# A second buffer for the blocks of RWKV's inverses, and the modulation's weights in pieces of 512 columns

## The chip, the cores and the metric

The kernel runs on one core of one Trainium2 chip. The metric is the device time of one execution in microseconds (us); the numbers given are medians over runs. A core has a matrix engine (PE), three engines for elementwise work (DVE, ACT, POOL), and a queue on SP that issues most of the transfers (DMA) between DRAM and the on-chip memory. Each engine, and SP too, takes its instructions in a fixed order: an instruction that waits holds back all that stand behind it on its engine.

## The reference, cut to what matters

A network of two layers over 1280 tokens (256 of context, 1024 of latents) of width 1024. For each layer:

```python
mod = silu(cond) @ ada_w[i] + ada_b[i]             # shifts, scales and gates: "the modulation"
h = rmsnorm(x, norm1_g) * (1 + sc1) + sh1
z = h @ w_in[i]                                    # split into four groups
mix = concat(s5(z0), rwkv7(z1), retention(z2), gla(z3)) @ w_out[i]
x = x + g1 * mix
x = x + g2 * (relu(rmsnorm(x, norm2_g) * (1 + sc2) + sh2) @ mlp_w1) ** 2 @ mlp_w2
```

`rwkv7` is a recurrence over tokens, forward and backward, in four heads of 64. Its step is `s = s * w + (s @ a) b^T + v k^T`, `y = s @ r`. In the first layer the modulation of the second layer's first part is computed as well.

## The kernel before, in words

A layer runs in stages: norm 1; the input projection (beside the parameters of S5 and its scans); **the mixers' stage**; output projection, norm 2 and MLP. In the trace the mixers' stage lies at about 462 to 1050 us (first layer) and 2498 to 3055 us (second layer). The rest is mostly dense matrix work.

In the mixers' stage three generators are interleaved by `merge`, each at a share of the matrix engine's estimated time: the modulation (`ada`), RWKV (`rw.run()`), and retention followed by the gated linear attention (`ret_run`, `gla_run`).

RWKV works in chunks of 128 tokens. A "pair" is one chunk forward and one backward; there are ten pairs in a layer. A pair enters `unit1` every six rounds (elementwise preparation, transposes, scores `TE` and `TO`), then `inv` is emitted for the pair, and twelve rounds after `unit1` comes `unit2`, so that `unit2` of one pair and `unit1` of the pair two places later are emitted side by side. `inv` solves 32 triangular blocks of 32x32. Its steps, with their lines:

- L514: four stores of blocks of `TE` and `TO` to a DRAM tile `S` (two buffers);
- L518: one load of `S`, four copies side by side, into the tile `B` (512 KB, **one buffer**);
- L523: a constant into `Yv` (two buffers);
- L527, L528: 31 steps of two small POOL instructions each, `rw_tmp <- rw_Yv, rw_B` and `rw_Yv <- rw_Yv, rw_tmp`;
- L531: four stores of `Yv` to a DRAM tile `S2`; L534: four loads of `S2` into `DT`, the inverse's blocks, which the first matmul of `unit2` (`psu <- rw_R, rw_DT`) multiplies by.

All these transfers stand in SP's queue, together with the loads of RWKV, retention, the gated linear attention and the modulation's weights.

`ada(i, q, pool, bufs)` makes 16 column tiles of the modulation: 8 rows of tiles by 4 column groups of 512. Each of its 16 steps (two for a row) loads one 128x1024 tile of `ada_w` (512 KB; L1517) into one of two buffers and runs two matmuls of 512 columns on it. In the mixers' stage `ada` is run three times in the first layer (48 steps) and twice in the second (32 steps). Its sums stay in the one PSUM bank of the kind `fi` until its last step.

The order on each engine is not that of the program's text: the program is built with `schedule_with_timeline_sim=True`, which lays out each engine's instructions by a simulated timeline. In the trace, instructions of `inv` on POOL alternate with those of the other generators.

Of the kernel before, what the change touches and what calls it, by code (L numbers as in the profile page):

```python
# [16 lines left out]
SEQ = 1024  # L17
# [9 lines left out]
def _consts():  # L27
# [44 lines left out]
    dt = (i[None, :] - i[:, None]).astype(f)            # t - s  # L72
# [9 lines left out]
    ang = np.stack([(tt // 64).astype(f)[:, None] * inv, (tt % 64).astype(f)[:, None] * inv], 1)   # [SEQ, 2, 16]  # L82
# [14 lines left out]
# per-layer small parameters, one column block each (layout only)  # L97
# [3 lines left out]
def _cols(a):  # L101
    """[n*128] -> [128, n]"""
    a = np.asarray(a)
    return np.ascontiguousarray(a.reshape(-1, 128).T)
# [19 lines left out]
def lay_s5(inp, i):  # L124
    """[128, 4*512+64]: B (re; im), B (im; re), C (re; im), C (im; re) by state, and d on the diagonal of its group"""
    g = lambda n: np.asarray(inp[n][i])
    br, bi = (g(n).transpose(2, 0, 1, 3).reshape(64, 512) for n in ("s5_b_re", "s5_b_im"))
    cr, ci = (g(n).transpose(3, 0, 1, 2).reshape(64, 512) for n in ("s5_c_re", "s5_c_im"))
    d = g("s5_d").reshape(4, 4, 16)
    dl = np.zeros((4, 32, 4, 16), np.float32)  # L130
    for p in range(16):
        dl[:, p, :, p] = d[:, :, p].T
    return np.concatenate([np.concatenate([a, b], 0) for a, b in ((br, bi), (bi, br), (cr, ci), (ci, cr))]
                          + [dl.reshape(128, 64)], 1)
# [13 lines left out]
class Pe:  # L148
    """the tensor engine, with an estimate of the time of what it was given (ns)"""
# [18 lines left out]
class K:  # L168
# [29 lines left out]
    def psum(self, **rings):  # L198
        """the banks of PSUM, shared out among kinds of users; b: the others"""
# [16 lines left out]
# ---------------------------------------------------------------- RWKV-7  # L216
def rw_mix(k, j, z, zm, mu, omu):
    """zm = z + mu*(shifted - z) for the 128 columns of tile j; z, zm [128, T]"""
# [42 lines left out]
RW_ROWS = 13            # rows of the spilled columns: v chunks swapped 2, kk 2, r 2, k 2, lo 1, v 2, v reversed by chunk 2  # L261


def rw_store(k, st, sm, omu, zrw, j, zt):
    """token shift of the 128 columns of tile j (zt [128, T]) and what the scans take from them, to DRAM;
    a generator: the parts that need the tensor engine come after the first step"""
# [45 lines left out]
class Rwkv:  # L312
    """zrw: DRAM [128, RW_ROWS, T] as rw_store leaves it; out(p, ps) takes the transposed output of 128 tokens"""

    R, LAT, NP = 6, 12, 3         # rounds between pairs, to their second part, pairs at a time
# [8 lines left out]
    def setup(self):  # L324
# [12 lines left out]
        # states and buffers with fixed zeros  # L337
# [15 lines left out]
        # by chunk: the first direction's output; what the normalized output is multiplied by, and what is added then  # L353
# [7 lines left out]
    def unit1(self, p, d, pr):  # L361
        """elementwise preparation, transposes, scores of 128 tokens in one direction"""
# [17 lines left out]
        def rev(ap):        # [.., 128] reversed in time for the backward direction  # L380
            return ap[..., ::-1] if d else ap

        def v4(ap):         # [128, 2, 128] -> [128, 2, c, 64]
# [11 lines left out]
        # V (scan order, chunks swapped), token-major, into its place beside the chunk updates  # L395
# [11 lines left out]
        ec = self.ec[u["n"] % 2]        # decay from a chunk's start to before and, one column later, after a token  # L407
# [3 lines left out]
        # ar: (r~ 0 | a~ 0 | a~ 1 | r~ 1); a~ in scan order, r~ in natural order within its chunk  # L411
# [6 lines left out]
        # bk: (b_ 0 | k_ 0 | k_ 1 | b_ 1); b = 2*kk*a (its factor -1/2 comes with the masks), k_d  # L418
# [7 lines left out]
        # r~ by keys, and the chunks' decays  # L426
# [13 lines left out]
        u["R"] = R = t("R", [128, 4, 2, 64], 5)      # (v | k) columns  # L440
        A.copy(R[:, :, 1, :], pv[:, 0:256].rearrange("p (h x) -> p h x", h=4))
        # scores: chunk 0 rows (b|k), columns (r~|a~); chunk 1 rows (k|b), columns (a~|r~)
        # TE: (end-of-chunk keys | r~ | a~), TO: (a~ | r~ | end-of-chunk keys)
# [5 lines left out]
        ps2 = [k.ps("u1"), k.ps("u1")]      # the halves of the array's rows work side by side  # L449
# [21 lines left out]
        # Aak V  # L471
# [9 lines left out]
    def gate(self, p, zin):  # L481
        """factor and addend of the normalized output, token-major: ln_g * g and (ln_b + bonus) * g"""
# [23 lines left out]
    def inv(self, pr):  # L506
        """(I - B)^-1 for strictly upper triangular 32x32 blocks: block (unit, head, block) on 4 partitions,
        rows i = 4 i' + j on the j-th"""
        k, nc, w = self.k, self.k.nc, self.w
        S = k.dram.tile([8, 4, 32, 32], F32, name="rw_S", bufs=2)      # (unit, head), block  # L510
# [5 lines left out]
        B = w.tile([128, 32, 32], F32, name="rw_B", bufs=1)  # L516
# [12 lines left out]
        S2 = k.dram.tile([8, 4, 8, 4, 32], F32, name="rw_S2", bufs=2)      # (unit, head), block, i', j, t  # L529
# [52 lines left out]
    def chain(self, u, act):  # L582
        """state pass and outputs of 128 tokens in one direction"""
# [52 lines left out]
    def run(self):  # L636
        """generator over the whole layer: in rounds, a pair of units (one in each direction) enters every R rounds and
        its second part LAT rounds later, when the inverses are there"""
# [27 lines left out]
def rr(gens, width=9):  # L666
    """round robin over generators, at most width at a time, in order; one that yields n sits out n rounds"""
# [17 lines left out]
def pipe(gens, R, width=9):  # L685
    """round robin over generators, of which one more enters every R rounds; one that yields n sits out n rounds"""
# [18 lines left out]
def rsqrt_small(k, y, x):  # L705
    """y = x^(-1/2) for tiles [128, 4], x > 0, without a table"""
# [3 lines left out]
def head_norm_gate(k, w, pre, py, g, lngh, out, p):  # L710
    """RMS norm over each head of py [128 tokens, 256] (PSUM), times ln_g and silu(g); lngh = ln_g/2"""
# [27 lines left out]
# ---------------------------------------------------------------- gated linear attention  # L739
class Gla:  # L740
    """DRAM: q [128 (head, key), T], alo [16, T], vg [T, 512] (v | g), and by chunk kc [128, NCH, 385]: keys times dk^-1/2 (given),
    sums of log decays (times 16; pb, one more column, and bf)"""
# [14 lines left out]
    def update(self, d, n, p, kh, v):  # L757
        """compact state of direction d after its n-th chunk p, from keys kh"""
# [16 lines left out]
    def expand(self, d, sc):  # L775
        """block diagonal over heads"""
# [5 lines left out]
    def chunk(self, p):  # L782
# [11 lines left out]
        if need:  # L794
            g = self.load("g", self.vg[tk, 256:512])
            L = t("L", [128, 14, 128], 2)          # exponents, then factors, of keys and queries by level
# [86 lines left out]
    def run(self):  # L883
# [6 lines left out]
        # log decays (times 16): min(y, 0) - ln(1 + exp(-|y|)), then prefix sums within chunks of 128:  # L890
        # bf inclusive, forward; pb exclusive, backward (one more column: the chunk's sum)
        self.bl, self.dec = t("bl", [128, 2, NCH]), t("dec", [128, 2, NCH])      # the chunks' decays and their exponents
# [33 lines left out]
# ---------------------------------------------------------------- retention  # L926
class Parts:
    """small tiles cut from one [128, n]"""
# [10 lines left out]
def ret_decays(k, w, dl, work):  # L939
    """log(sigmoid(dl)) for a tile [128, n] with equal rows: min(x,0) - 2*atanh(e/(2+e)), e = exp(-|x|)"""  # L940
# [5 lines left out]
    V.tensor_tensor(ax, ax, dl, op=OP.min)                  # -|x|  # L946
# [3 lines left out]
    V.tensor_tensor(u, u, e, op=OP.mult)                    # in [0, 1/3]  # L950
# [11 lines left out]
def exp_acc(k, work, out, x, pre):  # L962
    """exp(x) for small tiles to float32 accuracy, x clamped to [-87, 88]"""
# [19 lines left out]
def rope(k, st, x, p, o):  # L983
    """axial rotation of 128 latents' queries or keys x [128, 256] (4 heads) -> o"""
    V = k.nc.vector
    x = x.rearrange("p (h f a) -> p h f a", h=4, f=4)            # f: (half, x1|x2)
# [11 lines left out]
class Ret:  # L998
    """z: DRAM [T, 1024] (q | k | v | g), q and k rotated; dl [128, 8] decay logits (d, h)"""
# [13 lines left out]
    def update(self, d, n, kk, v):  # L1013
        """state of direction d (block diagonal by pair) before its chunk n+1"""
# [26 lines left out]
    def chunk(self, p):  # L1041
# [22 lines left out]
        AT = t("AT", [128, 2, 2, 128], 2)       # h2, pair  # L1064
# [22 lines left out]
    def run(self):  # L1087
# [12 lines left out]
        # decay within a chunk, both directions, times dk^-1/2: DM[s, h, t]  # L1100
# [9 lines left out]
        # factors of queries GQ[(h2, key), d, pair, t] = g^(t+1 | 128-t), of values GV[s, d, h] = g^(127-s | s)/8;  # L1110
        # gC[d, h] = g^128
# [15 lines left out]
        # states before the n-th chunk of a direction: [(h2, key), pair, (h2, v)], block diagonal in h2  # L1127
# [8 lines left out]
# ---------------------------------------------------------------- S5  # L1136
class S5:
    """u: DRAM [128 (s, p), 16, 160]: row p of each group at token 8c+s"""
# [14 lines left out]
    def params(self):  # L1153
        """state decays, powers, and the three matrices of 8-token steps, kept in DRAM"""
# [21 lines left out]
        V.tensor_scalar(sh, sh, 2.0, None, op0=OP.mult)             # 1 - cos  # L1176
# [5 lines left out]
        V.scalar_tensor_tensor(re, e1, 1.0, th, op0=OP.add, op1=OP.mult)        # expm1  # L1182
# [16 lines left out]
        # powers 0..8  # L1199
# [9 lines left out]
        # with the sign of the half: (-, +) and (+, -) of im; (+, -) of re  # L1209
# [9 lines left out]
        # unit phase of 8 steps, and its decay  # L1219
# [10 lines left out]
        # b_bar (re; im) and (im; re)  # L1230
# [15 lines left out]
        for d0 in range(0, 32, 4):  # L1246
# [26 lines left out]
            # lag matrices, group 4*gq + j at partitions 32j  # L1273
# [738 lines left out]
def merge(k, gens):  # L2012
    run(merged(k, gens))
# [41 lines left out]
```

## Time and profile before

| what | value |
|---|---|
| median of three runs | 3920.55 us (3920.0 to 3921.86) |
| span of the profiled execution, first to last instruction | 3930.7 us (its own time is given by this span alone) |
| PE busy | 3589.8 us (91%) |
| DVE, ACT, POOL busy | 2222.0, 1475.3, 1353.2 us (57%, 38%, 34%) |
| the chain that ended last | PE 64%, POOL 9%, DMA 9%, DVE 8%, ACT 5% |

The chain of waits is followed back from the last instruction: at each step to what released it, or to the instruction before it on its engine. Busy shares are means over stages with different limits; what a change in the mixers' stage is worth is to be read from that stage.

### The profile page before, as it was taken

Reading aid. Unit: us, or ns where it says so; the run is one execution under the profiler, and the core shown is the slowest. Engines: PE = TensorE matmul, PEld = TensorE weight load, DVE = VectorE, ACT = ScalarE, POOL = GpSimd, SP = SyncE. Lnnn points to the kernel's source line nnn. Section 1 sums busy time; section 2 is a strip of 40 time slices with the busy share of each in tenths; the row PEclk is TensorE's granted clock in tenths of the full one; section 3 lists DMA queues with packets and bytes.
Section 4 is the critical chain, followed back from the end, with each engine's and each line's share of the span. In section 5 each row is a group of like instructions: output and inputs, shape, how many; then the busy total and the mean of one; then the engine's idle time right before and its main releaser. Section 6 shows DMA issues by size and latency. Waiting matters only on the chain.

```text
span 3930.7 us, 61448 instructions
## 1 busy us (share of the span) xinstructions
PE 3589.8 (91%) x23136; PEld 2973.0 (76%) x23136; DVE 2222.0 (57%) x4654; ACT 1475.3 (38%) x2980; POOL 1353.2 (34%) x2690
## 2 busy tenths in 40 slices
PE   6999888888799999999998999788888799999997
PEld 2998766577687888888886987667677678888885
DVE  5875456667555444444448875555667464444445
ACT  4266345755433111111214365346655332111222
POOL 1541256567431111111111451266676321111112
PEclk8999988787799999999999999898778899999998
DMA  5434575532521111111103434663423411111111
GB/s 184 149 111 145 163 210 141 168 92 61 163 89 33 33 44 33 43 33 44 33 27 120 146 115 144 180 177 112 111 73 96 141 54 49 49 43 43 49 53 43
DMA packets 369241, 372.84 MB, mean 95 GB/s; under 512 B 97360, under 2 KB 313104, under 8 KB 368688
## 3 DMA queue, kind: packets, MB, share of 16 engines
q1 hardware_dynamic: 333600, 343.08, 28.8%
q10 hardware_dynamic: 35344, 25.83, 2.1%
q8 instruction: 183, 3.00, 0.3%
q14 instruction: 114, 0.93, 0.1%
HBM read 285.18 MB, written 83.63 MB: 94 GB/s over the span
## 4 chain that ended last, share of the span: by engine, by line
PE 64%; POOL 9%; DMA 9%; DVE 8%; ACT 5%; issue 3%; SPq 1%; ACTq 0%; DVEq 0%; POOLq 0%
PE psb L161 56%; PE psu L161 5%; POOL rw_Yv L528 3%; POOL rw_tmp L527 3%; DMA rw_B<-rw_S 2%; DMA rw_S<-rw_Yv 1%; PE pss L161 1%; PE psfi L161 1%; DMA ada_w<-in_ada_w_dram 1%; DVE s_W L1158 1%; PE psch L161 1%; DVE n_h L1579 1%; DMA gl_v<-z_gvg 1%; DVE w_lo L1478 1%; DVE zm L223 1%
## 5 line engine op out<-in xcount | busy, mean ns | idle before, releaser
L161 PE MATMUL psb<-hh,w_hi 128*128 128x512 f32 (+1 forms) x1784 | 664.6, 374 | 12.9 <-ACT hh L1951 4.5
L161 PE MATMUL psb<-hl,w_hi 128*128 128x512 f32 (+1 forms) x1784 | 662.5, 372 | 6.5 <-DVE hl L1581 6.5
L161 PE MATMUL psb<-hh,w_lo 128*128 128x512 f32 (+1 forms) x1784 | 659.5, 371 | 0.0
L161 PE MATMUL psb<-mh,w_hi 128*128 128x512 f32 (+1 forms) x1600 | 601.2, 377 | 20.1 <-ACT w_hi L1475 15.3
L161 PE MATMUL psb<-mh,w_lo 128*128 128x512 f32 (+1 forms) x1600 | 598.3, 375 | 6.6 <-DVE w_lo L1478 6.6
L161 PE MATMUL psb<-ml,w_hi 128*128 128x512 f32 (+1 forms) x1600 | 600.5, 375 | 0.0
L1932 DVE SCALAR_TENSOR_TENSOR x<-psb,mod,x 128x512 f32<-128x512 f32 (+1 forms) x640 | 436.9, 694 | 273.8 <-PE psb L161 273.0
L1478 POOL TENSOR_TENSOR w_lo<-w_raw,w_hi 128x1024 fp32r<-128x1024 f32 x84 | 215.0, 2560 | 765.2 <-ACT w_hi L1475 574.8
L1950 DVE TENSOR_TENSOR hr<-hr 128x512 f32<-128x512 f32 x160 | 150.5, 941 | 513.6 <-ACT hr L1949 513.5
L1949 ACT ACTIVATE hr<-psb 128x512 f32<-128x512 f32 x160 | 88.7, 555 | 862.7 <-PE psb L161 861.8
L161 PEld LDWEIGHTS psb<-hh,w_hi 128*128 128x128 f32 x1784 | 338.6, 190 | 77.7 <-issue 6.0
L161 PEld LDWEIGHTS psb<-hl,w_hi 128*128 128x128 f32 x1784 | 338.0, 190 | 72.7 <-DVE hl L1581 11.0
L161 PEld LDWEIGHTS psb<-hh,w_lo 128*128 128x128 f32 x1784 | 337.5, 189 | 61.2 <-issue 1.4
L1952 POOL TENSOR_TENSOR hl<-hr,hh 128x512 fp32r<-128x512 f32 (+1 forms) x80 | 95.3, 1191 | 795.0 <-ACT hh L1951 502.9
L161 PEld LDWEIGHTS psb<-mh,w_hi 128*128 128x128 f32 x1600 | 303.7, 190 | 81.1 <-ACT w_hi L1475 17.4
L161 PEld LDWEIGHTS psb<-mh,w_lo 128*128 128x128 f32 x1600 | 303.3, 190 | 67.9 <-DVE w_lo L1478 8.2
L161 PEld LDWEIGHTS psb<-ml,w_hi 128*128 128x128 f32 x1600 | 303.4, 190 | 60.3 <-issue 2.9
L1475 ACT CAST w_hi<-w_raw 128x1024 fp32r<-128x1024 f32 (+1 forms) x208 | 212.8, 1042 | 317.8 <-PE psb L161 268.5
L527 POOL TENSOR_TENSOR rw_tmp<-rw_Yv,rw_B 128x60 f32<-128x60 f32 (+24 forms) x620 | 206.1, 332 | 198.6 <-DMA rw_B<-rw_S 100.0
L161 PE MATMUL psb<-w_hi,hh 128*128 128x256 f32 (+1 forms) x928 | 266.0, 290 | 4.8 <-ACT w_hi L1475 4.7
L161 PE MATMUL psb<-w_lo,hh 128*128 128x256 f32 (+1 forms) x928 | 266.9, 288 | 0.6 <-DVE w_lo L1478 0.6
L161 PE MATMUL psb<-w_hi,hl 128*128 128x256 f32 (+1 forms) x928 | 266.2, 288 | 0.0
(469 smaller groups left out, 6710.2 us busy)
## 6 DMA issues: line engine op xcount, KB each, us to landing
w_raw<-in_mlp_w_dram SPq DMA_DIRECT2D x128, 512.0 KB, 3.6
ada_w<-in_ada_w_dram SPq DMA_DIRECT2D x96, 512.0 KB, 4.4
w_raw<-in_w_in_dram SPq DMA_DIRECT2D x40, 512.0 KB, 5.6
w_raw<-in_w_out_dram SPq DMA_DIRECT2D x32, 512.0 KB, 5.2
rw_zin<-z_rw SPq DMA_DIRECT2D x20, 576.0 KB, 5.9
rw_B<-rw_S SPq DMA_DIRECT2D x20, 512.0 KB
z_rw<-zm SPq DMA_DIRECT2D x14, 640.0 KB, 3.1
x<-in_xT_dram SPq DMA_DIRECT2D x4, 2048.0 KB
```

What stands on the lines that cost most here:

```text
L161: return self.t.matmul(out, lhsT, rhs, **kw)
L223: nc.vector.scalar_tensor_tensor(dst[p0:p1], src[p0:p1], mu[p0:p1, j:j + 1], dst[p0:p1], op0=OP.mult, op1=OP.add)
L527: eng.tensor_tensor(o, bc(Yv[:, 0:m, s:s + 1], [128, m, n]), bc(B[:, s:s + 1, s + 1:32], [128, m, n]), op=OP.mult)
L528: eng.tensor_tensor(Yv[:, 0:m, s + 1:32], Yv[:, 0:m, s + 1:32], o, op=OP.add)
L1158: T_ = lambda o, a, b, op: V.tensor_tensor(o, a, b, op=op)
L1475: nc.scalar.copy(hi[:, :n], raw[:, :n])
L1478: e.tensor_tensor(lo[:, :n], raw[:, :n], hi[:, :n].bitcast(F32), op=OP.subtract)
L1579: nc.vector.scalar_tensor_tensor(h, x[:, kt], g[:, kt, cond:cond + 1], r[:, :n], op0=OP.mult, op1=OP.mult)
L1932: V.scalar_tensor_tensor(self.x[b][:, dt_], ps[:, :n], mod[:, 40 + dt_, cnd:cnd + 1], self.x[b][:, dt_], op0=OP.mult, op1=OP.add)
L1949: A.activation(r[:, :n], ps[:, :n], AF.Relu)
L1950: V.tensor_tensor(r[:, :n], r[:, :n], r[:, :n], op=OP.mult)
L1952: (G if j else V).tensor_tensor(hl[:, j, :n], r[:, :n], hh[:, j, :n].bitcast(F32), op=OP.subtract)
```

## The change

`B` gets two buffers. `ada` gets a parameter `wide`, the columns of one loaded tile. At its old default of 1024 it does what it did (the first call, ahead of the layers, keeps it). In the mixers' stage it is called with 512: every matmul has its own tile and its own load of 256 KB, still in two buffers. A step still holds two matmuls, so it now holds two loads and uses both buffers. In on-chip memory `B` takes 4 KB more of each partition, and the `ada_w` tiles 4 KB less. The diff also takes out comments, which is left out here; two lines are added inside `ada`, so that lines behind it stand two further down.

```diff
-        B = w.tile([128, 32, 32], F32, name="rw_B", bufs=1)
+        B = w.tile([128, 32, 32], F32, name="rw_B", bufs=2)
...
-    def ada(self, i, q, pool, bufs=2):
+    def ada(self, i, q, pool, bufs=2, wide=1024):
...
                 if j % 2 == 0:
                     yield
-                    w = pool.tile([128, 1024], F32, name="ada_w", bufs=bufs)
+                if j * 512 % wide == 0:
+                    w = pool.tile([128, wide], F32, name="ada_w", bufs=bufs)
                     c = q * 2048 + j * 512
-                    nc.sync.dma_start(w, self.I["ada_w"][i, kt * 128:kt * 128 + 128, c:c + 1024])
-                k.pe.matmul(ps[32 * j:32 * j + 2, :], self.cs[:, kt], w[:, j % 2 * 512:j % 2 * 512 + 512],
+                    nc.sync.dma_start(w, self.I["ada_w"][i, kt * 128:kt * 128 + 128, c:c + wide])
+                o = j * 512 % wide
+                k.pe.matmul(ps[32 * j:32 * j + 2, :], self.cs[:, kt], w[:, o:o + 512],
                             start=kt == 0, stop=kt == 7)
...
-        merge(k, [(chain([self.ada(a, q, w, 2) for a, q in ad]), ADAW * len(ad)), ...
+        merge(k, [(chain([self.ada(a, q, w, 2, 512) for a, q in ad]), ADAW * len(ad)), ...
```

## Rows read from the trace of the kernel before

**Rows 1.** The page: span; the chain's share by line.

```profile
span 3930.7 us, 61448 instructions
...
PE psb L161 56%; PE psu L161 5%; POOL rw_Yv L528 3%; POOL rw_tmp L527 3%; DMA rw_B<-rw_S 2%; DMA rw_S<-rw_Yv 1%; PE pss L161 1%; PE psfi L161 1%; DMA ada_w<-in_ada_w_dram 1%; DVE s_W L1158 1%; PE psch L161 1%; DVE n_h L1579 1%; DMA gl_v<-z_gvg 1%; DVE w_lo L1478 1%; DVE zm L223 1%
```

**Rows 2.** Busy time by stretch: PE, PEld, DVE, ACT, POOL; clock; DMA share; GB/s.

```profile
462.00:1050.00 588.00, 491.34 (x4978) 392.56 (x4978) 386.03 (x1031) 319.72 (x862) 370.19 (x1002) 0.81 0.49 142
2498.00:3055.00 557.00, 454.92 (x4434) 372.86 (x4434) 357.26 (x939) 294.93 (x798) 345.34 (x950) 0.81 0.45 127
```

**Rows 3.** Waits, both stages: us in total, times, longest.

```profile
POOL rw_tmp L527 <- DMA rw_B<-rw_S: 43.1, 6, 9.0
...
POOL rw_tmp L527 <- DMA rw_B<-rw_S: 56.9, 8, 9.8
```

**Rows 4.** Chain of waits in order of time: start, us, what.

```profile
798.16 9.15 DMA rw_B<-rw_S
...
857.67 6.55 issue
...
899.79 9.21 DMA rw_B<-rw_S
...
954.43 8.93 DMA rw_B<-rw_S
...
2639.99 11.72 DMA rw_B<-rw_S
...
2828.85 10.54 DMA rw_B<-rw_S
...
2876.74 9.11 DMA rw_B<-rw_S
...
2980.97 9.92 DMA rw_B<-rw_S
```

**Rows 5.** SP's timeline: start, us; the scores' last stores ahead of those loads.

```profile
791.82 0.96 SPq L514 DMA_DIRECT2D rw_S<-rw_TO  x2
...
850.15 0.60 SPq L514 DMA_DIRECT2D rw_S<-rw_TO  x1
...
896.04 0.89 SPq L514 DMA_DIRECT2D rw_S<-rw_TO  x2
...
944.01 0.89 SPq L514 DMA_DIRECT2D rw_S<-rw_TO  x2
...
2606.41 0.89 SPq L514 DMA_DIRECT2D rw_S<-rw_TO  x2
...
2808.55 0.93 SPq L514 DMA_DIRECT2D rw_S<-rw_TO  x2
...
2870.71 0.93 SPq L514 DMA_DIRECT2D rw_S<-rw_TO  x2
...
2974.97 2.15 SPq L514 DMA_DIRECT2D rw_S<-rw_TO  x2
```

**Rows 6.** The scores' stores (line 514), first layer's stage: issue to landing.

```profile
DMA to landing us min/median/max: 2.2/4.1/6.4
```

**Rows 7.** Chain of waits: stores of the finished inverse, first, last and an undisturbed one.

```profile
563.27 6.91 DMA rw_S<-rw_Yv
...
2733.34 7.00 DMA rw_S<-rw_Yv
...
3022.44 2.21 DMA rw_S<-rw_Yv
```

**Rows 8.** The modulation, first layer's stage: its matmuls; transfers to landing; PE's wait.

```profile
L161 PE MATMUL psfi<-ada_w,condsl x192: 591/592/1061, 472.8 to 802.1; 128*2 128x512 f32 x192
...
ada_w<-in_ada_w_dram SPq DMA_DIRECT2D x48, 512.0 KB, 5.2
gl_v<-z_gvg SPq DMA_DIRECT2D x19, 128.0 KB, 2.2
...
PE psfi L161 <- DMA ada_w<-in_ada_w_dram: 8.6, 4, 6.5
```

More of the change, by code (lines that the diff above doesn't have):

```diff
@@ L1644, in layer @@
         ad = [(i, 1), (i, 2)] + ([] if last else [(i + 1, 0)])
-        merge(k, [(chain([self.ada(a, q, w, 2) for a, q in ad]), ADAW * len(ad)), (rw.run(), 165), (chain([self.ret_run(i, last), self.gla_run(i, last)]), 75)])
+        merge(k, [(chain([self.ada(a, q, w, 2, 512) for a, q in ad]), ADAW * len(ad)), (rw.run(), 165), (chain([self.ret_run(i, last), self.gla_run(i, last)]), 75)])
         w.release()
```

## The prediction

> **What bounds the kernel now.** I read the page first: the span is 3930.7 us, and 56% of the chain that ended last is dense matrix work (`psb`), which the diff does not touch. What it touches shows further down the same line: POOL's two instructions of the inverse at 3% each, the load `rw_B<-rw_S` at 2%, the store of the finished inverse at 1%, the modulation's weights at 1% [rows 1]. Then the view by stretches, for the two mixers' stages. PE is busy 491 of 588 us and 455 of 557, POOL 370 and 345, and no engine is full [rows 2]. PE's idle time, 97 + 102 = 199 us, is the most that the stages could give back while PE does the same work at the same clock. The granted clock has a mean of 0.81 of the full 2.4 GHz in both [rows 2]; I count nothing for a change in it.
>
> Then the waits. POOL waits 43.1 us in the first stage and 56.9 in the second, 14 times in all, for the load of `B` [rows 3]. With one buffer the load can be issued only when the last step of the inverse before has read `B`. The chain in order of time says which of these waits set the end: eight pieces, 9.15 + 6.55 + 9.21 + 8.93 + 11.72 + 10.54 + 9.11 + 9.92 = 75.1 us [rows 4]. The second of them is called "issue" there; it ends where POOL begins the next inverse, and I read it as one more such load. So this is a stage in which a transfer of some 9 us stands between one POOL inverse and the next, while POOL has nothing else that it may do, since its queue is in order.
>
> **Part 1: the second buffer of `B`.** No instruction is added. The load is now free to go as soon as the scores' stores have landed and the inverse two places before is done. How much earlier that is, SP's timeline tells: the last scores' store ends at 792.8, 850.8, 896.9, 944.9, 2607.3, 2809.5, 2871.6 and 2977.1 [rows 5], so 5.4, 6.9, 2.9, 9.5, 32.7, 19.4, 5.1 and 3.9 us before the eight pieces of [rows 4] begin. From each, 4.1 us go for the landing [rows 6]; the first stage's median stands for both. What is left, and no more than the piece itself, is 1.3 + 2.8 + 0 + 5.4 + 11.7 + 10.5 + 1.0 + 0 = 32.7 us. That is the lower bound, with every score arriving as late as now. The upper bound is all 75.1 us: the scores are themselves late because `unit1` is emitted beside the `unit2` of the pair two places before, which waits for that pair's inverse, so that an earlier inverse gives earlier scores. I take 45 us, nearer to the lower bound, because five of the eight leads are under 7 us: there the scores have to move first. It could go below the lower bound only if other work takes the place, which is a rival below.
>
> What is late next: the scores. On SP, the load will then wait at the head of the queue for their stores instead of for POOL. Behind it stand the loads of the other mixers and the stores of the previous inverse; the wait is the 4.1 us of [rows 6] at most, and today's wait for POOL is of the kind of [rows 3], so I count nothing for it.
>
> **Part 2: the stores of the finished inverse.** Today `B`'s 512 KB are issued at the same moment as the four small stores of the previous inverse, because both wait for the same last POOL instruction. Five times such a store is on the chain, 6.91 us in the first and 7.00 us in the last of them, about 7.8 us on the mean [rows 7]. After the very last inverse, with no load beside it, the piece is 2.21 us [rows 7]. A load that went earlier leaves the stores alone: up to 5 x 5.6 = 28 us, and nothing if the loads move only by a few us and meet them again. I take half, 14 us, because the early inverses, where these pieces lie, are the ones with long leads, but some of them are followed by stretches of PE and ACT work that do not hurry. Part 2 never adds time by itself.
>
> **Part 3: pieces of 512 columns.** Bytes and matmuls stay the same. The 80 steps of the two stages get 80 more loads on SP. The important thing is the cover. With two buffers of a whole step each, a load is issued about two steps ahead; with both buffers used in one step, it is issued when the same half of the step before is done, one step ahead. In the first stage 48 steps lie between 472.8 and 802.1 us [rows 8], so 329.3 / 47 = 7.0 us apart on the mean. Two matmuls take 2 x 0.6 us, and 512 KB land in 5.2 us [rows 8]: a cover of 14.0 - 1.2 - 5.2 = 7.6 us today. A load of 256 KB is not in the rows; it must lie between the 2.2 us of 128 KB and the 5.2 us of 512 KB [rows 8], and I take the middle, 3.7 us. The new cover is 7.0 - 1.2 - 3.7 = 2.1 us: still positive, but the steps are not evenly spaced, and PE waits 8.6 us for these weights already today [rows 8]. Lower bound of the cost: nothing, because the generator is finished at 802 us, well before the first stage's end at 1050 [rows 2, 8], and may slip, and SP's extra issues fit in its idle time. Upper bound: every one of the 80 steps waits for the landing, 80 x 3.7 = 296 us, far off. I take as much again as PE waits now, scaled to 80 steps: 8.6 x 80 / 48 = 14 us.
>
> The Trainium skill, "DMA: Bandwidth & Descriptors", section "Measured (HBM→SBUF, 128 partitions, SWDGE, issued from GpSimd)", speaks against this part: batch transfers to 1 MiB or more, since small ones pay a fixed price. By its fit in "Anatomy of one DMA — SWDGE (gpsimd) path" (2.0 us and the bytes at 436 GB/s) a 256 KB load would take 2.6 us, an estimate that would make the cover 3.2 us; the rows show 5.2 us for 512 KB, where the fit would say 3.2 us, so I go by the rows.
>
> **Sum.** 45 + 14 - 14 = 45 us less. Against the profiled execution that is 3930.7 - 45 = 3885.7 us of span; its span is 10.2 us above the median of the runs, 3920.55 us, and I carry the difference over: **3875.5 us**. A difference under 0.2% (7.8 us) is about what a measurement of this kernel can't tell from no change. By the bounds of parts 1 to 3 without the far end of part 3, the forecast's own range is 32.7 + 0 - 14 = 19 to 75 + 14 - 14 = 75 us less: 3846 to 3902 us.
>
> **The rivals.**
>
> *The modulation runs dry (slower).* The second tile in flight is what hides a load now. If the planner leaves steps close together on PE, each with its matmuls at PE's head, a step waits up to 3.7 us, and all mixers wait with it. It decides from (45 + 14) / 3.7 = 16 of the 80 steps on. With 20 of them: 74 us lost, 59 us gained, 3920.55 + 15 = 3936 us. For it: PE's 8.6 us today with twice the depth, and weights on the chain at 1% [rows 1, 8]. Against it: the mean cover is positive, and only four waits make up the 8.6 us. The rule of the Trainium skill on batching ("DMA: Bandwidth & Descriptors", as above) points this way. Chance 0.15.
>
> *The load was not what the stage waited for (no change).* The scores come as late as now, and PE, ACT and DVE between the inverses take up what POOL gains. Then only the two pieces with long leads, 11.7 + 10.5 us, are gained, and the 14 us of part 3 go against them: 3920.55 - 8 = 3912 us, at the edge of what can be told. For it: four leads of 5.4 us or less [rows 4, 5]. Against it: POOL's instructions lie on both sides of most of these pieces, and 6% of the whole chain is theirs [rows 1]. Chance 0.12.
>
> *Everything is given back (much faster).* The scores move up with the inverses, stores and loads no longer meet, and the modulation slips without harm: 75 + 28 = 103 us, 3817 us. For it: 199 us of idle PE [rows 2] leave room. Against it: the leads. Chance 0.15.
>
> The forecast keeps 0.58. The chances by sign follow: faster 0.58 + 0.15 = 0.73, the same 0.12, slower 0.15. The range takes in the much faster case and the unchanged one, 3815 to 3928 us, and leaves out 0.15 for the slower one and a little at the other end.
>
> **What would show it.** Right: POOL's wait for `rw_B` falls from 100 us to under 45 in sum; the pieces `rw_B<-rw_S` leave the chain or shrink; the stores of the inverse land in under 5 us; the stages are shorter by some 20 us each, and every other stage has its old length. Wrong: PE's wait for `ada_w` grows beyond 30 us; or POOL waits as long as before, now behind the scores' stores; or the simulated timeline orders the engines so differently that stages of RWKV, retention and linear attention overlap in another way. This last can go to either side by more than part 2 or 3, and I know no row to price it.

## The result, and the profile after

The changed kernel takes 3959.76 us (median of 4 runs, 3944.43 to 3966.31), the kernel before beside it 3921.2 us: a ratio of 1.0092 [1.0069, 1.0116], so 38.6 us (under 1%) slower where 45 less were forecast. The profiled span grew by 27.9 us. The page of the changed kernel, its span, busy times and chain by engine:

```profile
span 3958.6 us, 61536 instructions
...
PE 3625.6 (92%) x23136; PEld 2955.7 (75%) x23136; DVE 2218.0 (56%) x4654; ACT 1478.0 (37%) x2982; POOL 1339.8 (34%) x2690
...
PE 67%; DVE 8%; DMA 8%; POOL 6%; ACT 5%; issue 4%; SPq 1%; ACTq 0%; DVEq 0%; POOLq 0%
```

The two mixers' stages of the changed kernel, columns as in [rows 2]:

```profile
465.00:1068.00 603.00, 508.64 (x4978) 378.31 (x4978) 387.12 (x1033) 316.86 (x859) 364.01 (x1004) 0.85 0.48 139
2516.00:3085.00 569.00, 478.11 (x4434) 367.87 (x4434) 353.65 (x939) 300.52 (x802) 340.75 (x950) 0.81 0.45 124
```

Against [rows 2] the stages are 15 and 12 us longer, which is the whole difference. PE has the same numbers of matmuls and is busy 17 and 23 us longer, in the first stage at a granted clock of 0.85 in place of 0.81. Its idle time in the two stages, from which alone a gain could come, fell from 199 us to 185. So the loss lies in PE's busy time, and not in its waits. POOL's busy time, the inverses in it, is about what it was.

The chain by line, in tenths of a per cent, of the kernel before:

```profile
by line: PE psb L161 56.2%; PE psu L161 4.5%; issue 3.1%; POOL rw_Yv L528 2.7%; POOL rw_tmp L527 2.6%; DMA rw_B<-rw_S 2.1%; DMA rw_S<-rw_Yv 1.1%; PE pss L161 1.1%; PE psfi L161 1.0%; DMA ada_w<-in_ada_w_dram 0.9%; DVE s_W L1158 0.8%; PE psc
```

and of the changed one:

```profile
by line: PE psb L161 56.9%; PE psu L161 5.2%; issue 3.7%; DMA ada_w<-in_ada_w_dram 2.2%; PE psfi L161 2.2%; POOL rw_Yv L528 1.9%; POOL rw_tmp L527 1.7%; DMA rw_B<-rw_S 1.2%; PE pss L161 1.1%; DVE s_W L1158 0.8%; PE psch L161 0.7%; PE psu L1
```

The modulation, its weights' loads and its matmuls (`psfi`), had 1.9% of the chain, 75 us, and has 4.4%, 174 us. POOL's two steps and the load of `B` had 7.4%, 291 us, and have 4.8%, 190 us. That the two nearly cancel doesn't show which edit moved what. In the kernel before at another share of RWKV (160, an experiment below), with one buffer and whole tiles, the chain has moved the same way, with 2.9% for the modulation, 2.5% for POOL's two steps, and less for the load of `B` than any line shown here:

```profile
by line: PE psb L161 56.5%; PE psu L161 5.7%; issue 3.3%; DMA ada_w<-in_ada_w_dram 1.6%; DMA rw_S<-rw_Yv 1.3%; POOL rw_Yv L528 1.3%; PE psfi L161 1.3%; POOL rw_tmp L527 1.2%; PE pss L161 1.0%; PE psch L161 1.0%; DVE s_W L1158 0.8%; DMA gl_c
```

**What the matmuls of the modulation cost.** PE's timeline, start and duration, matmuls of the modulation alone. Each matmul leaves two records. The kernel before:

```profile
500.98 1.03 PE L161 MATMUL psfi<-ada_w,condsl 128*2 128x512 f32 x4
503.91 1.03 PE L161 MATMUL psfi<-ada_w,condsl 128*2 128x512 f32 x4
```

The changed one:

```profile
504.44 1.02 PE L161 MATMUL psfi<-ada_w,condsl 128*2 128x512 f32 x2
...
508.51 1.02 PE L161 MATMUL psfi<-ada_w,condsl 128*2 128x512 f32 x2
...
510.54 1.02 PE L161 MATMUL psfi<-ada_w,condsl 128*2 128x512 f32 x2
```

Before, the two matmuls of a step (four records) took 1.03 us together. Now one (two records) takes 1.02 us by itself, with other matmuls between it and its neighbour; the granted clock is 1.00 in both stretches. So the two, next to each other on PE, ran side by side. They write different partitions of the sums (`ps[32 * j:32 * j + 2]`) and multiply by two columns each. That fits the Trainium skill, "TensorEngine Tiling (Array Packing)", section "Tiling Modes": independent tiles of the array can run matmuls in parallel. In which mode the array ran, the trace doesn't show. The pieces took most of the pairs apart: each matmul now has a load of its own to wait for, and other matmuls are laid out between them. Of the 160 matmuls of the two stages 7 ran without another of their kind beside them before; in the changed kernel 100 do. The same matmuls over both stages, in a view by line (count | busy us, mean ns | idle before), before:

```profile
L161 PE MATMUL psfi<-ada_w,condsl 128*2 128x512 f32 x320 | 85.9, 649 | 11.8 <-DMA ada_w<-in_ada_w_dram 11.6
```

and after:

```profile
L161 PE MATMUL psfi<-ada_w,condsl 128*2 128x512 f32 x320 | 153.5, 665 | 38.6 <-DMA ada_w<-in_ada_w_dram 38.3
```

The duration of one record hardly changed (649 and 665 ns); the time in which PE is busy with them went up by 67.6 us, and PE's wait for their weights by 26.7 us.

**The inverses.** POOL's timeline at the seam of two inverses; each begins with the step of 31 columns and ends with that of 8. The changed kernel:

```profile
613.59 0.21 POOL L528 TENSOR_TENSOR rw_Yv<-rw_Yv,rw_tmp 128x8 f32<-128x8 f32 x1
613.88 0.24 POOL L527 TENSOR_TENSOR rw_tmp<-rw_Yv,rw_B 128x31 f32<-128x31 f32 x1
...
849.57 0.21 POOL L528 TENSOR_TENSOR rw_Yv<-rw_Yv,rw_tmp 128x8 f32<-128x8 f32 x1
851.43 1.03 POOL L707 TENSOR_TENSOR gl_nrs<-gl_ns,mhalf 128x4 f32<-128x4 f32 x1 [1.66 <-DVE gl_ns L720]
864.83 0.24 POOL L527 TENSOR_TENSOR rw_tmp<-rw_Yv,rw_B 128x31 f32<-128x31 f32 x1 [12.36 <-issue]
```

At 614 us no time lies between two inverses; before, it was 8 to 17 us at every one of the nine seams of the first layer. Over the nine seams of the changed kernel it is 0, 0, 3, 4, 16, 35, 15, 21 and 21 us: the buffer does what it is for in the first half of the stage, and nothing in the second; the sum even grew, from 97 to 116 us. In the second layer seven of the nine seams shrank, four of them to 0, and the sum fell from 100 to 59 us; but the ten inverses themselves, each from its first instruction to its last, took 420 us where they had taken 372 (other work on POOL stands between their steps). What held the late seams of the first layer, SP's timeline of the same kernel shows in one case:

```profile
845.26 1.00 SPq L514 DMA_DIRECT2D rw_S<-rw_TO  x2
849.80 1.24 SPq L531 DMA_DIRECT2D rw_S<-rw_Yv  x2
851.15 0.53 SPq L754 DMA_DIRECT2D gl_v<-z_gvg  x1
851.73 1.45 SPq L531 DMA_DIRECT2D rw_S<-rw_Yv  x2
853.30 0.56 SPq L518 DMA_DIRECT2D rw_B<-rw_S  x1
```

The last scores are sent at 845, some 4 us before the inverse before is done at 849.8, and the load of `B` stands behind that inverse's own stores (line 531) on SP. That cost it some 3.5 us at most, by an estimate: with the 4.1 us of [rows 6] the scores themselves land at about 850. At the other four late seams the scores are sent 2 to 25 us after the inverse before has ended. The chain of the changed kernel (start, us, what) ahead of the longest seam:

```profile
794.00 1.16 PE psu L161 x8
795.16 0.95 PE psfi L161 x2
796.11 1.09 PE psu L161 x8
797.20 0.95 PE psfi L161 x2
798.15 0.89 PE psu L161 x16
...
800.08 0.42 DVE rw_ES L575
800.55 1.72 DMA rw_S<-rw_TO
802.36 8.37 DMA rw_B<-rw_S
```

Two lone matmuls of the modulation, 0.95 us each, stand on this chain. But they don't stand ahead of the scores. The timelines of PE and DVE name what ran:

```profile
791.34 1.16 PE L161 MATMUL psu<-rw_ar,rw_bk 64*128 64x128 f32 x8
...
794.00 1.16 PE L161 MATMUL psu<-rw_TE,rw_EL 128*128 128x128 f32 x8 [0.40 <-DVE rw_EL L565]
...
797.34 0.41 DVE L459 TENSOR_TENSOR rw_TO<-psu,c_rwm 128x256 f32<-128x256 f32 x1
```

The scores' own matmuls (`psu<-rw_ar,rw_bk`) had ended at 792.5; DVE wrote the last scores at 797.75, and their stores went out by 801. The matmuls from 794 on are `unit2` of an earlier pair, which reads scores. The profile puts the last store down to an instruction of that `unit2` (line 575). So what makes the scores late isn't shown, and that the modulation's matmuls do it isn't either.

### The profile page after: what moved, and what is told of

The parts are those of the page before. It is cut to its first block, busy times and chain, and to the rows that moved or that the text cites. A ratio compares the mean times of both kernels' runs of the same rounds, so it can differ in the third digit from the quotient of the medians.

```text
span 3958.6 us, 61536 instructions
## 1 busy us (share of the span) xinstructions
PE 3625.6 (92%) x23136; PEld 2955.7 (75%) x23136; DVE 2218.0 (56%) x4654; ACT 1478.0 (37%) x2982; POOL 1339.8 (34%) x2690
## 4 chain that ended last, share of the span: by engine, by line
PE 67%; DVE 8%; DMA 8%; POOL 6%; ACT 5%; issue 4%; SPq 1%; ACTq 0%; DVEq 0%; POOLq 0%
PE psb L161 57%; PE psu L161 5%; DMA ada_w<-in_ada_w_dram 2%; PE psfi L161 2%; POOL rw_Yv L528 2%; POOL rw_tmp L527 2%; DMA rw_B<-rw_S 1%; PE pss L161 1%; DVE s_W L1158 1%; PE psch L161 1%; PE psu L165 1%; DMA n_h<-z_mix 1%; DVE w_lo L1478 1%; DVE n_h L1581 1%; DVE zm L223 1%
## 5 line engine op out<-in xcount | busy, mean ns | idle before, releaser
L527 POOL TENSOR_TENSOR rw_tmp<-rw_Yv,rw_B 128x60 f32<-128x60 f32 (+24 forms) x620 | 199.1, 321 | 151.6 <-issue 52.6
```

The source lines that it names most:

```text
L527: eng.tensor_tensor(o, bc(Yv[:, 0:m, s:s + 1], [128, m, n]), bc(B[:, s:s + 1, s + 1:32], [128, m, n]), op=OP.mult)
```

## The experiments

All times are medians with the ratio to the kernel before on the same chip and its 95% interval. The edits are against the kernel before where the text says so, else against the changed one. Two tables at the end set sums of the traces beside each other.

**One part at a time.** The pieces alone; against the changed kernel:

```diff
-        B = w.tile([128, 32, 32], F32, name="rw_B", bufs=2)
+        B = w.tile([128, 32, 32], F32, name="rw_B", bufs=1)
```

> One buffer for B as before, the modulation's weights in pieces of 512 in two buffers. Theory depth (the modulation's loads are issued only one step ahead, and that costs more than the second buffer of B gives): slower than the changed kernel or like it, 3955 to 4000 us. Theory order (the second buffer of B itself, by the new order of the engines, is what slows the stages): 3921 us, within 8. Theory count (80 more transfers on SP and the DMA engines, however deep the buffers): 3945 to 3990 us.

Measured: 3989.15 us, 1.0167 [1.0152, 1.0182], 65 us slower. The pieces by themselves lose more than the pair of changes; the buffer takes 29 us off this (26 with each kernel set against the runs of the kernel before beside it).

The buffer alone needs 4 KB of each partition that the pieces had freed. Room was made in other places, here against the kernel before; the control has the same edits with one buffer.

```diff
-        self.consts(self.const, ("ident", "bones", "ones", "sgn"))
+        self.consts(self.const, ("ident", "ones", "sgn"))
...
-        B = w.tile([128, 32, 32], F32, name="rw_B", bufs=1)
+        B = w.tile([128, 32, 32], F32, name="rw_B", bufs=2)
...
-        tmp = w.tile([128, 256], F32, name="rw_tmp", bufs=1)
+        tmp = w.tile([128, 76], F32, name="rw_tmp", bufs=1)
...
-        AD = t("AD", [128, 4, 32], 1)
+        AD = LK[:, 0].rearrange("p (h t) -> p h t", h=4)
...
-        r = pool.tile([128, 512], F32, name="ada_r", bufs=1)
+        r = pool.tile([128, 1024], F32, name="ada_w", bufs=bufs)[:, 0:512]
...
+        k.consts(st, ("bones",))
```

> Two buffers for B, the modulation's weights in tiles of 1024 columns in two buffers as before. Room is made elsewhere (the POOL temporary cut to its used width, the modulation's last tile taken from the ring of its weights, two small tiles moved). Depth and count: faster than before, 3870 to 3905 us. Order: 3945 us or more.

> The kernel before with the room made elsewhere and nothing else: the control of the two runs with more memory. All theories: 3921 us, within 10. Where it lies elsewhere, the two runs are read against it.

Measured: 3945.53 us, 1.0055 [1.0041, 1.007] with two buffers, 3976.26 us, 1.0135 [1.0115, 1.0155] for the control. Against its control the buffer gains 31 us; the edits that make room lose 52. One of these edits by itself, the modulation's last tile taken from the ring of the weights (against the kernel before):

```diff
-        r = pool.tile([128, 512], F32, name="ada_r", bufs=1)
+        r = pool.tile([128, 1024], F32, name="ada_w", bufs=bufs)[:, 0:512]
```

> The kernel before with the modulation's last tile taken from the ring of its weights, which was one of the edits of the control at 3976 us. For a while one of the two buffers is not there for the next weights. Depth: a part of the control's 52 us, 3935 to 3976 us. If the rest of the control's edits did it: 3921 us, within 10. Any order: anywhere.

Measured: 3949.73 us, 1.0076 [1.006, 1.0091], 28 us slower, with nothing added or removed but one small tile's place.

**The look-ahead.** Four buffers of 512 columns hold as much ahead as two of 1024. With one buffer for `B`, and with two (the second with the edits for room):

```diff
-        merge(k, [(chain([self.ada(a, q, w, 2, 512) for a, q in ad]), ADAW * len(ad)), ...
+        merge(k, [(chain([self.ada(a, q, w, 4, 512) for a, q in ad]), ADAW * len(ad)), ...
```

> One buffer for B, the weights in pieces of 512 columns in four buffers: the memory of the kernel before, as many bytes ahead, 80 more transfers, nothing else touched. Depth: 3921 us, within 10 (the pieces in two buffers were at 3989). Count: 3960 us or more. Third theory, any order (the planner lays the engines out anew at the smallest change, and the order of the kernel before is a lucky one): anywhere between 3920 and 3990 us.

> Two buffers for B, pieces of 512 columns in four buffers: as many bytes ahead as before, twice as many transfers; the same room made as in the run with the buffer alone. Depth: 3870 to 3905 us. Count: 3945 us or more. Order: 3945 us or more.

Measured: 3970.29 us, 1.0116 [1.0096, 1.0136], and 3949.34 us, 1.0064 [1.0048, 1.0081]. PE's wait for the weights is back to 10.7 us in the first, and it still loses 49 us (its profiled execution took 3953.45 us, the fastest of its runs). So the halved look-ahead isn't needed for most of the loss. Beside the buffer, four pieces take 4 us more than two tiles of 1024 (3945.53 us), less than the intervals tell, though PE is busy 42 us longer with their matmuls: not all of that time lies on the path. PE's timeline of the first of them shows the pairs only partly together:

```profile
501.69 1.02 PE L161 MATMUL psfi<-ada_w,condsl 128*2 128x512 f32 x2
503.73 1.02 PE L161 MATMUL psfi<-ada_w,condsl 128*2 128x512 f32 x2
505.05 1.03 PE L161 MATMUL psfi<-ada_w,condsl 128*2 128x512 f32 x4
```

**The order.** The shares of `merge` change no work, only where the planner puts it. Against the kernel before, each alone: `ADAW` 9 or 11, RWKV's share 160, the share of retention and linear attention 77.

```diff
-ADAW = 8
+ADAW = 9
...
-ADAW = 8
+ADAW = 11
...
-        merge(k, [... (rw.run(), 165), (chain([self.ret_run(i, last), self.gla_run(i, last)]), 75)])
+        merge(k, [... (rw.run(), 160), (chain([self.ret_run(i, last), self.gla_run(i, last)]), 75)])
...
-        merge(k, [... (rw.run(), 165), (chain([self.ret_run(i, last), self.gla_run(i, last)]), 75)])
+        merge(k, [... (rw.run(), 165), (chain([self.ret_run(i, last), self.gla_run(i, last)]), 77)])
```

> The kernel before with the modulation's share in the merge 9 instead of 8 (ADAW): the same instructions, tiles and buffers, another interleaving. Depth and count: 3921 us, within 10. Any order: more than 15 us away from it, most likely slower.

> The kernel before with the modulation's share 11 instead of 8 (with 9 the order on PE, POOL and SP stayed what it was). Order: slower, 3940 to 3985 us. Pieces and buffers: 3921 us, within 10.

> The kernel before with RWKV's share in the merge 160 instead of 165. No instruction, tile, buffer or transfer differs, only the order in which the generators emit. If the order of the kernel before is a favourable one and any new order costs: slower, 3940 to 3985 us. If the cost came with the pieces and the ring of their buffers: 3921 us, within 10.

> The kernel before with the share of retention and linear attention 77 instead of 75: a third new order with nothing else changed; it keeps more of the old order on POOL than the other two. Order: slower, 3930 to 3970 us. That shares 160 and eleven were bad settings for other reasons than the new order: 3921 us, within 10.

Measured: `ADAW` 9 leaves the order of POOL, SP and PE (without the dense `psb`) as it was, name by name, and takes 3921.01 us, 0.9994 [0.9984, 1.0004]. The other three lay the engines out anew and take 3965.17 (1.0116 [1.0103, 1.0129]), 3964.78 (1.011 [1.0097, 1.0123]) and 3931.61 us (1.0024 [1.0013, 1.0035]): 43, 43 and 9 us slower for the same work. The last keeps more of the old order than the others. The longest sequence that its 2690 instructions on POOL have in common with the old one (same operation, names and shape) has 2446, against 2392 and 2346; in the changed kernel it has 2245. The two that lose 43 us also ran at a lower granted clock, 0.919 and 0.920 in their profiled executions against 0.932 with `ADAW` 9; so their 43 us are longer waits and a lower clock together (second table below). The same three shares in the changed kernel, and `ADAW` 16:

> The changed kernel with the modulation's share 11. Order: anything from -40 to 40 us from the kernel before with the same share. Pieces and buffers: 30 to 50 us above it.

> The changed kernel with RWKV's share 160. Order: the difference from the kernel before with the same share is not the 38 us of the shares as they were, but anything from -40 to 40 us. Pieces and buffers: 30 to 50 us above the kernel before with the same share.

> The changed kernel with the share 77. The change is worth some 20 us in an order that was not chosen: 10 to 30 us below the kernel before with the same share, 3920 to 3955 us. That the two gains of 17 and 22 us were chance: from 40 us above to 60 us below it.

> The changed kernel with the modulation's share 16 instead of 8: its steps are emitted twice as far apart, so that one step ahead covers a load. Depth: faster than the changed kernel, 3900 to 3940 us. Count: as the changed kernel, 3950 to 3970 us. Any order: anywhere.

Measured: 3943.57 (1.0063 [1.0047, 1.0079]), 3947.36 (1.0063 [1.0051, 1.0076]), 3951.67 (1.008 [1.0066, 1.0094]) and 3995.59 us (1.0197 [1.0176, 1.0218]). Share by share the change is worth -22, -17 and +20 us, and +39 at the shares that both kernels have. The gain seen at two neutral settings wasn't there at the third. `ADAW` 16 runs the modulation at another pace and loses 36 us against the changed kernel.

**No simulated timeline.** Built without it, the engines keep the order in which the program emits. The kernel before, the pieces with one buffer, four pieces with one buffer, and the whole change:

```diff
-    with _tile.TileContext(nc, schedule_with_timeline_sim=True) as tc, ExitStack() as ctx:
+    with _tile.TileContext(nc, schedule_with_timeline_sim=False) as tc, ExitStack() as ctx:
```

> The kernel before, its instructions laid out without the simulated timeline (schedule_with_timeline_sim=False): another order on every engine, the same work. It is the base for the three runs beside it. All theories: slower than 3921 us, by 0 to 200 us.

> As the run before it, with pieces of 512 columns in two buffers and one buffer for B. If the pieces in two buffers cost by waits that any order meets: 40 to 80 us above the base without the timeline, as with it (65 us). If the loss came from how the planner lays out the changed program: not the same size, from -20 to 30 us.

> Pieces of 512 columns in four buffers, one buffer for B, without the simulated timeline: the bytes ahead of the base and twice the transfers. If the number of transfers costs: 30 to 60 us above the base. If the planner's order was the cause of the 49 us with the timeline: within 20 us of the base.

> The changed kernel without the simulated timeline. If the second buffer of B gives some 30 us in any order, as it did twice with the timeline: 20 to 40 us below the run with pieces alone. If these gains are chance: anything between 30 us above it and 60 us below it.

Measured: 4201.06 (1.0702 [1.0685, 1.0718]), 4222.62 (1.0753 [1.0731, 1.0775]), 4212.44 (1.073 [1.0708, 1.0752]) and 4219.2 us (1.0747 [1.0731, 1.0763]). So the pieces cost 22 us here, four of them 11, which the intervals hardly tell from nothing, and the buffer gains 3 us, less than they tell. The second and the last have the same order name by name on POOL, SP and PE (without `psb`): the only pair in which the buffer was tried with nothing else moved. The first and the second share more than nine tenths of it (2530 of POOL's 2684, the modulation's left out).

But these four runs can tell little of the sizes with the timeline, since much of what the edits act on isn't there. PE's wait for the inverse's blocks over the whole execution, with the pieces and one buffer, and the same with two buffers (us in total, times, longest):

```profile
PE psu L161 <- DMA rw_DT<-rw_S: 0.9, 1, 0.9
```

With the timeline it is 53.8 us in the kernel before. A buffer that brings the inverse earlier had nothing to give here. And 45 of the 160 matmuls of the modulation stand alone already without the pieces (7 with the timeline), 86 with them, so that their busy time grows by 40 us, from 124.0 to 163.8, in place of 69.

The sums, both stages together (440 to 3110 us; `ADAW` 16, whose stages are longer, to 3140): PE busy with the modulation's matmuls; PE's wait for its weights; POOL's wait ahead of the inverses' step of line 527, whatever released it; PE's wait for the inverse's blocks `DT`.

| kernel | buffers of `B`, of weights | matmuls | for weights | POOL, line 527 | for `DT` |
|---|---|---|---|---|---|
| before | 1, 2 x 1024 | 85.9 | 11.6 | 157.8 | 53.8 |
| share 9 / 11 / 160 / 77 | 1, 2 x 1024 | 84.5 / 87.4 / 90.3 / 82.8 | 10.3 / 15.3 / 25.2 / 15.0 | 161.4 / 183.7 / 146.0 / 154.9 | 55.1 / 49.6 / 36.2 / 51.4 |
| room alone / last tile in ring | 1, 2 x 1024 | 87.4 / 86.7 | 24.5 / 16.4 | 170.8 / 157.4 | 56.5 / 45.3 |
| four pieces | 1, 4 x 512 | 123.2 | 10.7 | 143.1 | 51.9 |
| pieces alone | 1, 2 x 512 | 154.7 | 40.6 | 153.9 | 40.0 |
| buffer alone | 2, 2 x 1024 | 95.0 | 44.2 | 114.0 | 21.8 |
| buffer, four pieces | 2, 4 x 512 | 137.0 | 37.3 | 81.2 | 27.6 |
| changed | 2, 2 x 512 | 153.5 | 38.3 | 110.5 | 24.6 |
| changed, share 11 / 160 / 77 | 2, 2 x 512 | 164.7 / 153.7 / 154.7 | 53.7 / 43.6 / 46.9 | 77.0 / 97.2 / 90.8 | 14.6 / 6.0 / 14.6 |
| changed, share 16 | 2, 2 x 512 | 167.9 | 39.8 | 117.0 | 16.6 |

Whatever order the simulated timeline gave, two buffers of `B` take PE's wait for `DT` from 36 to 57 us down to 6 to 28, and POOL's from 143 to 184 down to 77 to 117; and two pieces of 512 take the matmuls from 83 to 95 us up to 154 to 168. Both effects belong to the edits, not to the order.

PE's busy and idle time over the whole profiled execution (idle is the span less the busy time; the ends of matmuls are modelled in a profile), and the mean granted clock:

| kernel | span | PE busy | PE idle | clock |
|---|---|---|---|---|
| before | 3930.7 | 3589.8 | 340.9 | 0.926 |
| before, share 9 (the same order) | 3919.3 | 3569.7 | 349.6 | 0.932 |
| pieces alone | 3982.5 | 3624.0 | 358.5 | 0.931 |
| changed | 3958.6 | 3625.6 | 333.0 | 0.931 |
| before / changed, share 11 | 3973.0 / 3940.7 | 3603.6 / 3626.5 | 369.4 / 314.2 | 0.919 / 0.937 |
| before / changed, share 160 | 3965.1 / 3945.6 | 3591.9 / 3615.9 | 373.2 / 329.7 | 0.920 / 0.936 |
| before / changed, share 77 | 3933.6 / 3942.1 | 3573.6 / 3607.1 | 360.0 / 335.0 | 0.927 / 0.939 |

The first two rows are the same order at two clocks: PE's busy time differs by 20 us. So the changed kernel is best set against share 9, whose clock is like its own:

```profile
PE 3569.7 (91%) x23136; PEld 2957.6 (75%) x23136; DVE 2223.6 (57%) x4654; ACT 1473.7 (38%) x2980; POOL 1345.9 (34%) x2690
```

PE is busy 56 us longer and idle 17 us less, together the 39 us of the result. The pieces alone, at the same clock, make PE busy 54 us longer and idle 9 us longer; the buffer then takes 26 us off the idle time and nothing off the busy time. At the other three shares the change has the same two signs: busy 23, 24 and 34 us longer, though at a higher clock, and idle 55, 44 and 25 us less.

## Why the prediction was wrong

**Part 3 failed first, at "Bytes and matmuls stay the same".** The number of matmuls does; their time doesn't. I priced a step at 2 x 0.6 us from the duration of one record [rows 8], where the view by line, shown above, has 85.9 us busy for 320 records of 649 ns, 208 us if they ran one after the other. A busy time of less than half of count times mean is what work side by side looks like; the two records of one matmul overlap too, but far less (1.02 us for two of 0.59). The term of 14 us is the growth of PE's wait, which came out at 26.7 us; the 67.6 us of PE time were left out. At like clocks PE's whole busy time grew by 56 us, more than the 39 us lost. What both come to in the time: 65 us for the pieces alone. The 22 us without the simulated timeline are no second measure of it, since many pairs were apart there before. That the shorter cover makes the wait was judged rightly: with it restored, the wait was 10.7 us, and 49 of the 65 us remained. A clock that changes was put at nothing as well; in the first stage it rose from 0.81 to 0.85, and PE's matmuls other than the modulation's were busy 431 us there in place of 448, which hid part of the cost.

**Part 1 failed at "an earlier inverse gives earlier scores".** POOL's wait put down to the load fell from 100.0 to 40.3 us, under the 45 named, but its wait called "issue" rose from 6.6 to 52.6; all its waits ahead of line 527 went from 157.8 to 110.5. On the chain of the changed kernel the load remains:

```profile
802.36 8.37 DMA rw_B<-rw_S
...
852.28 12.55 issue x2
...
913.59 9.42 issue
...
976.50 10.19 DMA rw_B<-rw_S
...
2912.75 6.74 DMA rw_B<-rw_S
2919.49 2.30 issue
...
2957.34 5.76 DMA rw_B<-rw_S
...
3007.57 3.07 DMA rw_B<-rw_S
3010.64 6.44 issue
```

The pieces called "issue" end where POOL begins an inverse. Together (the first load of a layer, which no buffer frees, left out) these are 64.8 us where [rows 4] have 75.1: 10 less, not 45; with the chains moving as they do with the order, this is a rough measure. In the first layer POOL stopped waiting in the first half of the stage, where its wait didn't set the end, and waited longer in the second. The step itself can be read in the middle of the first layer. The fifth and the sixth inverse end 19 and 23 us earlier than before. The end of the sixth, before:

```profile
798.22 0.21 POOL L528 TENSOR_TENSOR rw_Yv<-rw_Yv,rw_tmp 128x8 f32<-128x8 f32 x1
```

and after, with the last stores of the next scores:

```profile
775.42 0.21 POOL L528 TENSOR_TENSOR rw_Yv<-rw_Yv,rw_tmp 128x8 f32<-128x8 f32 x1
...
799.74 1.25 SPq L514 DMA_DIRECT2D rw_S<-rw_TO  x2
```

These scores went out at 791.82 before [rows 5], so they came 8 us later, behind inverses that came earlier. Why they are late stays open; the modulation's matmuls, which now go on to 949.6 us in place of 802.1 [rows 8], are not shown to be the reason. I had counted five of eight leads under 7 us and still took more than the lower bound. (That bound took 4.1 us of landing for both stages; the second stage's own median is 1.7 us, which would raise it by some 5 us.) The buffer alone came out at a gain of 31 us against its control and 29 beside the pieces, and it is PE's idle time that fell; both pairs also differ in their order, so these are no clean prices. Where nothing else moved it was 3 us, in an order in which PE didn't wait for the inverse.

**Part 2 held, as far as the chain tells.** On the chain the stores of the finished inverse are five pieces again, of the changed kernel these:

```profile
1028.33 2.04 DMA rw_S<-rw_Yv
...
2622.39 3.96 DMA rw_S<-rw_Yv
...
2670.28 1.97 DMA rw_S<-rw_Yv
...
2883.45 1.96 DMA rw_S<-rw_Yv
...
2964.40 2.19 DMA rw_S<-rw_Yv
```

Their 12.1 us stand where the 5 x 7.8 us of [rows 7] stood: 27 us less, close to the upper bound of the term. The five of the prediction left out a sixth piece of the kernel before, and the one after the last inverse wasn't among them:

```profile
2594.08 3.52 DMA rw_S<-rw_Yv
```

All seven came to 44.8 us, so the fall is 33 us. At share 77 it is from 57 to 15 us.

**The order, which had no price, has one now.** I held the sum against an order that the change doesn't leave alone: 2245 of POOL's 2690 instructions keep their sequence. Settings that change no work lose 9, 43 and 43 us when the engines are laid out anew, and nothing in the one case when they weren't. So the order of the kernel before is a good one among its neighbours, and an edit that has the stage laid out anew is likely to lose it. The sum forecast a gain in an order that no longer existed. At three other shares the change comes out at -22, -17 and +20 us, so its own worth isn't settled in sign. Its two halves are: in all four pairs PE is busy longer and idle less, and which of the two is larger turns with the order.

Of the rivals, the dry modulation named the right side and the right place, but its mechanism (the cover) is the smaller part: with the cover restored, 49 of 65 us remained. Of what the prediction would have taken for wrong, PE's wait for `ada_w` beyond 30 us came true, and so did the new order. But two signs of being right came true as well, POOL's wait for `rw_B` under 45 us and the inverse's stores under 5 us on the chain, and the stages were longer all the same. These signs were about waits, and PE's busy time had no sign.

What stays open: how much of the idle time belongs to the buffer and how much to the order, since the two moved together; what in the old order is good, since no single wait accounts for the 43 us of a neutral share, and part of it is the clock; and what the 80 more transfers cost by themselves, or whether a load cut in two whose matmuls still stand side by side would gain. This last wasn't tried. No version ran faster than the kernel before; the nearest ones with two buffers took 3944 to 3949 us (ratios of 1.0055 to 1.0064).

## What to carry to other kernels

Before an edit separates two matmuls, compare the busy time of their group with count times mean, and look at the timeline: if two take as long as one, they run side by side, and separating them doubles their cost on that engine. A second buffer frees a load from its last reader only; read how early its source is written, and what stands ahead of it in the queue, before its wait is counted as a gain. A chain of waits tells where the end was set in one execution; that a line left it doesn't tell which edit did it. Set PE's busy and idle time apart, at like clocks, to see on which side an edit acts. Where a planner lays out the engines anew with every edit, measure the edit at several settings that change no work, and take the spread between them for the size of what one comparison can tell.

## What the runs showed that I had not expected

- Two matmuls of 512 columns with two columns of weights, into different partitions of one bank, take 1.03 us together and 1.02 us each alone.
- A share that changes no work moves this kernel by up to 43 us (1.1%), over five times the 7.8 us that the prediction took for what a measurement can't tell; with the order unchanged the ratio is 0.9994 [0.9984, 1.0004].
- Without the simulated timeline the kernel takes 7% more (4201.06 us), and the edits move the time less, 22 us for the pieces in place of 65: more pairs are apart there to begin with, and PE doesn't wait for the inverse.
- A transfer that a second buffer makes free can still wait for the same event through its queue: the load of 853.30 us stood behind the stores of the very inverse whose end it no longer needed. Here that cost little, if the estimate above holds that the scores landed at about the same time.
- The same order name by name, at a granted clock of 0.926 and 0.932 in two executions, leaves PE's busy time 20 us apart (3589.8 and 3569.7 us), half of what this change moved.
